# Modulation rows of a two-layer diffusion backbone: up to two per weight granule in four projection blocks, none beside attention

## The chip, the cores and the metric

One core of one Trainium2 chip runs the whole kernel. The metric is the device time of one execution in microseconds (us). TensorE (PE) does the matrix products, VectorE (DVE) and ScalarE (ACT) the elementwise work, GpSimd (POOL) some of it, and SyncE (SP) issues the transfers between HBM and the core's own memory. Each engine works through its own instructions in order, and SP issues its transfers in order.

## The reference

Two layers over 512 latent tokens of width 2048, and 256 context tokens. All data is f32.

```python
m = silu(cond) @ ada_w + ada_b            # adaLN: [2048] x [2048, 3 * 2048]
sh, sc, gt = split(m, 3)
h = rms_norm(x, g) * (1 + sc) + sh
# even layer: one projection h @ w_in into u, v, gates, q, k, v; context gives k and v only
ya = chunk_gmlp(gelu(u), gelu(v)) * silu(ag)         # A: spatial mixing in chunks of 128 tokens
yb = diff_attention(q, [k, kc], [v, vc]) * silu(bg)  # B: 8 heads, two softmaxes each, one subtracted
x = x + gt * (concat(ya, yb) @ w_out)
# odd layer, with its own adaLN: h @ w_in, GLU, depthwise convolution of 31 taps, LayerNorm, gate, w_out
```

The change concerns the adaLN vectors that are not needed at once: the even layer's `gt`, and the odd layer's scale, `sh` and `gt`.

## The kernel before, in words

Every product is taken in three passes, because operands are split into a high half (rounded for TensorE) and a low half (the rest): high by high, high by low, low by high. A **weight granule** is 1 MB of a weight matrix. `load_w` (L98) issues its load on SP into `raw` (three buffers, L94), makes the high half `whi` on ScalarE (L103) and the low half `wlo` on VectorE or GpSimd (L104); each of the two has two buffers, so `whi` of a granule waits until TensorE has left the granule two before it.

The stages, in the names used below:

- **K0**: the first half of K, by 512 columns, while the first adaLN vectors are computed on TensorE and the normalised inputs `hf`, `hcf` are split into `hhi`, `hlo` and `hc`.
- **V0, K1, V1, Q0, Q1**: halves of V, K and Q by `m_block` (L170). Four granules each; K and V have 72 matmuls a granule (latent and context tokens), Q has 48. Each block's results go through `qk_post` (L513: norm and rotation, `ms`, `tn`, `rot`, then a transpose `z` and the split `qkhi`, `qklo`) or `v_post` (L550), and are written to HBM (`k_s`, `v_s`, `q_s`).
- **AV0, AV1**: the gMLP's value half; behind each, `spatial_weights` (L632) transposes four of the eight spatial matrices `wsr` into `z` (L635) and splits them.
- **U**: two groups of `t_group` (L115); behind each, the spatial mixing, whose gated result `mx` (L679) is written to `ug_s` (L680).
- **Attention** (L898 on): 32 turns of scores `S`, maxima, exponentials `e` (L841), transposes `t`, split into `ph` and `pl` (L854, through L111 and L112), and values `oT` (L864). Its order on TensorE is written by hand: 18 granules of the remaining projections (`fill_stream`, L722) are spread between the turns. `load_kq` (L796) loads `kk` and `qq`.
- **Out-projection** and then the odd layer.

**Modulation rows.** The four late vectors are sums over 64 rows of 1 MB (`raw`, 128 x 2048), sixteen for each. `ada_step` (L452) is called by a hook once per granule: it loads a row through `load_raw` and adds it, times a column of `silu_c`, to the sum `acc` on VectorE (L468; the first row of a vector by L466). After the sixteenth, the vector is spread over the partitions (`spread`), turned into columns (`columns`) and, where needed, written out as a row (`row`), one of these at each later call. `hook` takes one row, `hook2` up to two. Before the change the 64 rows lie so: four in each of V0, K1, V1 and Q0, three in Q1, eight in AV, thirteen in U, thirteen beside attention, eleven in the out-projection.

A scheduler puts the instructions of each engine in an order from the program's order and its own estimates; loads and halves of weights get priority (`W_AHEAD`). TensorE's order is written by hand in K0 and attention, SP's in K0.

Of the kernel before, what the change touches and what calls it, by code (L numbers as in the profile page):

```python
# [45 lines left out]
def hybrid_layers_kernel(  # L46
# [43 lines left out]
    y_s = dscr([2, KT, P, T], "y_s")  # L90


    def load_raw(W, r0, nk, c0, ncols):
        raw = wp.tile([P, nk, ncols], F32, tag="raw", bufs=3, name=nm("raw"))  # L94
        SP.dma_start(raw, W[r0 : r0 + nk * P, c0 : c0 + ncols].rearrange("(k p) n -> p k n", p=P))
        return raw

    def load_w(W, r0, nk, c0, ncols, lo_eng=None):  # L98
        with tc.high_priority(offset=W_AHEAD):
            raw = load_raw(W, r0, nk, c0, ncols)  # L100
            hi = wp.tile([P, nk, ncols], F32R, tag="whi", name=nm("whi"))
            lo = wp.tile([P, nk, ncols], F32R, tag="wlo", name=nm("wlo"))
            A.copy(hi, raw)  # L103
            (lo_eng or V).tensor_tensor(lo, raw, hi.bitcast(F32), op=ALU.subtract)  # L104
        return hi, lo
# [256 lines left out]
    def make_hc(kt, Acol, shcol):  # L362
        z = zt(TC)
        for t in range(NTC):
            PE.transpose(z[:, t * P : (t + 1) * P], cch[t][kt // 4][:, (kt % 4) * P : (kt % 4 + 1) * P], ident)
        hcf = tp.tile([P, TC], F32, tag="d", name=nm("hcf"))
        A.activation(hcf, z, AF.Identity, bias=shcol[:, 1:2], scale=Acol[:, 1:2])
        hc = hcp.tile([P, 2, TC], F32R, tag="hc", name=nm("hc"))
        split(hc[:, 0, :], hc[:, 1, :], hcf, V)
        hcm[kt] = (hc[:, 0, :], hc[:, 1, :])  # L370
# [4 lines left out]
    k0ps = [psA.tile([P, 512], F32, tag="m", name=nm("mb")) for _ in range(NT + NTC)]  # L375

    with tc.manual_schedule(engines={mybir.EngineType.PE, mybir.EngineType.SP}):
        wks = {0: load_w(e_w_in, 0, 4, C_K, 512)}
        for q in range(4):
            ada_load(0, q)  # L380
        work = []
# [1 line left out]
        for j in range(NS):  # L383
# [21 lines left out]
            for q in range(4):  # L405
                if j + 1 < NS:
                    ada_load(j + 1, q)
                    if j == 0 and q == 3:
                        load_ctx()
                    if q == 2 and sets[j][-1] % 4 == 3 and sets[j][-1] < KT - 1:  # L410
                        wks[sets[j][-1] // 4 + 1] = load_w(e_w_in, (sets[j][-1] + 1) * P, 4, C_K, 512)
                if q == 3:
                    work += now
                for f in work[: 3 + q % 2]:
                    f()
                del work[: 3 + q % 2]
# [30 lines left out]
    for W, c0, kind in ((e_ada_w, 2 * D, 0), (o_ada_w, D, 1), (o_ada_w, 0, 2), (o_ada_w, 2 * D, 3)):  # L447
        for jt in range(KT):
            ada_jobs.append((W, c0, kind, jt))
    ada_state = {"i": 0, "acc": None}  # L450

    def ada_step(zalloc, n=1):  # L452
        if ada_tail:
            f = ada_tail.pop(0)
            f(zalloc)
            if f.__name__ == "spread":
                return
        for _ in range(n):
            if ada_state["i"] >= len(ada_jobs):
                return  # L460
            W, c0, kind, jt = ada_jobs[ada_state["i"]]
            ada_state["i"] += 1
            raw = load_raw(W, jt * P, 1, c0, D)[:, 0, :]
            if jt == 0:
                ada_state["acc"] = ap_.tile([P, D], F32, tag="acc", name=nm("acc"))
                V.tensor_scalar(ada_state["acc"], raw, sc_[:, 0:1], None, op0=ALU.mult)  # L466
            else:
                V.scalar_tensor_tensor(ada_state["acc"], raw, sc_[:, jt : jt + 1], ada_state["acc"], op0=ALU.mult, op1=ALU.add)  # L468
            if jt == KT - 1:
                ada_tail.extend(ada_finish(kind, ada_state["acc"]))  # L470
                return
# [41 lines left out]
    def qk_post(ps, which, tt, half, tok0, dst, rope):  # L513
# [25 lines left out]
        z = zt()  # L539
        for i in range(4):  # L540
            PE.transpose(z[:, i * P : (i + 1) * P], r[:, i * P : (i + 1) * P], ident)
        hi = tp.tile([P, 4, P], F32R, tag="hi", name=nm("qkhi"))
        lo = tp.tile([P, 4, P], F32R, tag="lo", name=nm("qklo"))
        split(hi, lo, z.rearrange("p (a b) -> p a b", b=P))
        for s, tl in ((0, hi), (1, lo)):
            SP.dma_start(
# [1 line left out]
            )  # L548

    def v_post(ps, half, tok0):  # L550
        hi = tp.tile([P, 4, P], F32R, tag="hi", name=nm("vhi"))
        lo = tp.tile([P, 4, P], F32R, tag="lo", name=nm("vlo"))
        split(hi, lo, ps.rearrange("p (a b) -> p a b", b=P))
        for s, tl in ((0, hi), (1, lo)):
            SP.dma_start(
                v_s[4 * half : 4 * half + 4, s, tok0 : tok0 + P, :].rearrange("h t d -> t h d"), tl.bitcast(F32)
            )
# [9 lines left out]
    def q_done(ps, half):  # L567
        for b in range(NT):
            qk_post(ps[b], 0, b, half, b * P, q_s, True)

    hook, hook2 = (lambda gi, n=n: ada_step(zt, n) for n in (1, 2))
    k_done(k0ps, 0)
    ps = m_block(e_w_in, C_BV, both(), psA, "m", hook)
    v_done(ps, 0)


# [32 lines left out]
        V.tensor_scalar(lam, lam, LAMBDA_INIT, None, op0=ALU.add)  # L609
        V.tensor_scalar(nlam, lam, -1.0, None, op0=ALU.mult)  # L610

    ps = m_block(e_w_in, C_K + 512, both(), psA, "m", hook)
    k_done(ps, 1)
    ps = m_block(e_w_in, C_BV + 512, both(), psA, "m", hook)
    v_done(ps, 1)
    for hb in range(2):
        ps = m_block(e_w_in, C_Q + 512 * hb, lat(), psA, "m", hook)
        q_done(ps, hb)
    p12a.close()

# [21 lines left out]
    for hb in range(2):  # L642
        ps = m_block(e_w_in, C_AV + 512 * hb, lat(), psA, "m", hook)
        for t in range(NT):
            av_ = avt[t][:, 512 * hb : 512 * hb + 512]
            A.activation(av_, ps[t], AF.Gelu)
            junk = bp.tile([P, 512], F32, tag="mx", name=nm("junk"))
            A.activation(junk, av_, AF.Square, accum_out=ssv[:, t, hb : hb + 1])
        spatial_weights(hb)
    vn = []  # L650
    for t in range(NT):
        hi = bp.tile([P, AW], F32R, tag="wv", bufs=9, name=nm("vnh"))
# [5 lines left out]
        V.scalar_tensor_tensor(lo, avt[t], rsv[:, t : t + 1], hi.bitcast(F32), op0=ALU.mult, op1=ALU.subtract)  # L658
        vn.append((hi, lo))

    for ug in range(2):
        ps = t_group(e_w_in, C_U + 512 * ug, hm, psA, "m", hook=hook2)
        for j in range(4):
            g = 4 * ug + j
            gu = bp.tile([P, T], F32, tag="gu", bufs=3, name=nm("gu"))
# [56 lines left out]
    def fill_stream():  # L722
# [10 lines left out]
        for x, (n, gi) in enumerate(grans):  # L733
            kind, i = jobs[n][:2]
            w, nxt = nxt, (load(*grans[x + 1]) if x + 1 < len(grans) else None)
            if gi == 0:
                ps = ps0 if kind == "y" else [None, None]
            if x % 4 != 3:
                ada_step(zt3, 1)
            if (n, gi) == (7, 1):  # L740
                for kt in [0, 1, 2, 3, 4, 5, 8]:
                    y_load(kt)
# [514 lines left out]
```

## Time and profile before

| | us |
|---|---|
| median of three runs | 1892.61 (1892.12 to 1898.86) |
| the profiled execution | 1892.11 |
| its span | 1890.3 |
| TensorE busy | 1819.3 |
| VectorE busy | 1125.1 |
| ScalarE, GpSimd busy | 560.2, 446.7 |
| rows added on VectorE by L468 (60) | 145.2 |

The profile is of one execution; 1.8 us lie around its span. In its rows, a line such as "L468 DVE ... acc<-raw" names the line of the kernel, the engine, the tile written and the tiles read. A bracket at the end of a timeline row tells how long the engine stood idle before the row, and what released it. In the list of waits the numbers are the total in us, the number of waits and the longest. In a row of windows the columns are the window's length, busy us and number of instructions of PE, PE's weight loads, DVE, ACT and POOL, then TensorE's granted clock as a share of full speed, the transfer engines' busy share and GB/s.

### The profile page before, as it was taken

How to read it: one execution, taken by the hardware profiler on the slowest of the kernel's cores; microseconds unless marked ns; L12 is line 12 of the kernel's file. 1: busy time of each engine (PE TensorE's matmuls, PEld its weight loads, DVE VectorE, ACT ScalarE, POOL GpSimd, SP SyncE). 2: the span in 40 equal slices, each digit the busy share in tenths (PEclk: the TensorE clock that was granted, in tenths of full speed). 3: DMA queues.
4: the chain of work that ended last, by engine and by line, in shares of the span. 5: the costliest groups of instructions: out<-in, count | busy, mean ns of one | idle time of the engine just before them, and what ended most of it. 6: DMA issues, size and time to landing. Idle time of an engine off the chain costs nothing.

```text
span 1890.3 us, 21892 instructions
## 1 busy us (share of the span) xinstructions
PE 1819.3 (96%) x8767; PEld 1486.8 (79%) x8767; DVE 1125.1 (60%) x1571; ACT 560.2 (30%) x747; POOL 446.7 (24%) x173
## 2 busy tenths in 40 slices
PE   5999999999999987999999999999999999999998
PEld 2568888888788866877788879888888888888887
DVE  4437436357553645666685555329999999865111
ACT  3332112122331233444343224422222222364110
POOL 0002001011000121323220002135445445444432
PEclk9999999999999998999999999999999999999999
DMA  9996745656763875664676763222332322323441
GB/s 323 339 328 211 220 144 171 197 160 225 249 233 104 319 207 178 186 179 142 203 287 204 252 209 115 89 90 90 99 102 90 106 95 89 101 101 133 141 155 61
DMA packets 208487, 327.34 MB, mean 173 GB/s; under 512 B 10249, under 2 KB 116610, under 8 KB 200194
## 3 DMA queue, kind: packets, MB, share of 16 engines
q1 hardware_dynamic: 208386, 325.94, 53.6%
q8 instruction: 69, 1.13, 0.2%
q14 instruction: 32, 0.26, 0.0%
HBM read 292.33 MB, written 33.58 MB: 172 GB/s over the span
## 4 chain that ended last, share of the span: by engine, by line
PE 75%; DMA 10%; DVE 6%; issue 4%; ACT 2%; POOL 1%; SPq 1%; DVEq 0%; ACTq 0%; POOLq 0%
PE tg L67 28%; PE mb L67 19%; PE m L67 14%; PE fm L67 5%; DMA raw<-in_o_ada_w_dram 4%; DVE acc L468 2%; PE oT L67 2%; DVE wlo L104 2%; PE z L304 2%; PE S L67 2%; ACT whi L103 1%; DMA raw<-in_e_w_in_dram 1%; POOL wlo L104 1%; DMA q_s<-qklo 1%; DMA raw<-in_e_ada_w_dram 1%
## 5 line engine op out<-in xcount | busy, mean ns | idle before, releaser
L104 POOL TENSOR_TENSOR wlo<-raw,whi 128x2048 fp32r<-128x2048 f32 x80 | 369.3, 4616 | 670.2 <-ACT whi L103 662.7
L103 ACT CAST whi<-raw 128x2048 fp32r<-128x2048 f32 x136 | 259.8, 1910 | 720.8 <-PE tg L67 205.4
L1122 DVE SCALAR_TENSOR_TENSOR z<-y,dwc,z 128x512 f32<-128x512 f32 x480 | 319.4, 754 | 0.1
L67 PE MATMUL tg<-h2h,wlo 128*128 128x512 f32 x704 | 274.7, 390 | 0.0
L67 PE MATMUL tg<-h2l,whi 128*128 128x512 f32 x704 | 273.9, 389 | 0.0
L67 PE MATMUL tg<-h2h,whi 128*128 128x512 f32 x704 | 270.8, 389 | 0.0
L468 DVE SCALAR_TENSOR_TENSOR acc<-raw,silu_c,acc 128x2048 f32<-128x2048 f32 x60 | 145.2, 2420 | 132.6 <-DMA raw<-in_o_ada_w_dram 85.0
L104 DVE TENSOR_TENSOR wlo<-raw,whi 128x2048 fp32r<-128x2048 f32 x56 | 128.2, 2290 | 140.5 <-ACT whi L103 140.5
L67 PE MATMUL mb<-whi,hhi 128*128 128x512 f32 x512 | 203.1, 398 | 0.0
L67 PE MATMUL mb<-whi,hlo 128*128 128x512 f32 x512 | 201.6, 394 | 0.0
L67 PE MATMUL mb<-wlo,hhi 128*128 128x512 f32 x512 | 201.5, 394 | 0.0
L67 PEld LDWEIGHTS tg<-h2h,wlo 128*128 128x128 f32 x704 | 132.2, 188 | 27.9 <-issue 0.5
L67 PEld LDWEIGHTS tg<-h2l,whi 128*128 128x128 f32 x704 | 132.2, 188 | 27.9 <-issue 0.5
L67 PEld LDWEIGHTS tg<-h2h,whi 128*128 128x128 f32 x704 | 132.2, 188 | 27.3
L194 POOL TENSOR_TENSOR rs<-ms,mhalf 128x8 f32<-128x8 f32 x20 | 38.2, 1923 | 375.1 <-DVE ms L193 375.1
L67 PEld LDWEIGHTS mb<-whi,hhi 128*128 128x128 f32 x512 | 97.1, 190 | 32.1 <-issue 11.7
L67 PEld LDWEIGHTS mb<-whi,hlo 128*128 128x128 f32 x512 | 97.1, 190 | 20.3
L67 PEld LDWEIGHTS mb<-wlo,hhi 128*128 128x128 f32 x512 | 97.0, 190 | 19.4 <-DVE wlo L104 0.2
L67 PE MATMUL fm<-hhi,whi 128*128 128x512 f32 x256 | 109.3, 427 | 0.0
L67 PE MATMUL fm<-hlo,whi 128*128 128x512 f32 x256 | 102.8, 402 | 0.0
L67 PE MATMUL fm<-hhi,wlo 128*128 128x512 f32 x256 | 102.6, 401 | 0.0
L67 PE MATMUL m<-wlo,y2h 128*128 128x512 f32 x256 | 99.6, 389 | 0.0
(265 smaller groups left out, 3021.6 us busy)
## 6 DMA issues: line engine op xcount, KB each, us to landing
raw<-in_e_w_in_dram SPq DMA_DIRECT2D x56, 1024.0 KB, 5.9
raw<-in_o_ada_w_dram SPq DMA_DIRECT2D x48, 1024.0 KB, 6.2
raw<-in_o_w_in_dram SPq DMA_DIRECT2D x48, 1024.0 KB, 5.1
raw<-in_e_ada_w_dram SPq DMA_DIRECT2D x64, 512.0 KB, 8.0
raw<-in_e_ada_w_dram SPq DMA_DIRECT2D x16, 1024.0 KB, 5.2
raw<-in_e_w_out_dram SPq DMA_DIRECT2D x16, 1024.0 KB, 5.2
raw<-in_o_w_out_dram SPq DMA_DIRECT2D x16, 1024.0 KB, 6.1
qq<-q_s SPq DMA_DIRECT2D x16, 512.0 KB, 7.9
```

Source lines behind the costliest of these rows:

```text
L67: return PE.matmul(o, l, r, start=start, stop=stop)
L103: A.copy(hi, raw)
L104: (lo_eng or V).tensor_tensor(lo, raw, hi.bitcast(F32), op=ALU.subtract)
L194: G.tensor_tensor(dst, tmp, mhalf[:, 0:1].broadcast_to([P, n]), op=ALU.pow)
L304: PE.matmul(ada_ps[j][32 * g : 32 * g + 32, 0 : 2 * nc_], S[:, kt, :], raw[:, i, :], start=(kt < 4), stop=(kt >= KT - 4), skip_group_check ...
L468: V.scalar_tensor_tensor(ada_state["acc"], raw, sc_[:, jt : jt + 1], ada_state["acc"], op0=ALU.mult, op1=ALU.add)
L1122: V.scalar_tensor_tensor(zi if t == TAPS - 1 else z, y2[:, t : t + T], w(t), z, op0=ALU.mult, op1=ALU.add)
```

## The change

`ada_step` is parted into taking a row (`ada_take`, which issues its load) and adding it (`ada_add`). With a pool given, a call first adds the row taken ahead in the call before, then takes and adds its own row, and then takes one more, into a pool `w0` that has a single buffer; that row is added at the next call. `hook0` does so in V0, K1, V1 and Q0; Q1 and AV keep one row a granule, U up to two, and attention has none. V1 has the last sum of the first vector and its steps, so that only two of its granules take two rows. The 64 rows now lie so: eight in V0 and in K1, four in V1, eight in Q0, four in Q1, seven in AV, thirteen in U, none beside attention, twelve in the out-projection.

To find room for `w0`, the high and low halves of `qk_post` and `v_post` share three buffers where they had two each, `rb` is put among them, and `hcf` shares a tag with `hf`. K0's weights load through `w0` as well. `spatial_weights` is called behind the first two granules of the first U group, no longer behind the AV blocks.

```diff
-    def load_raw(W, r0, nk, c0, ncols):
-        raw = wp.tile([P, nk, ncols], F32, tag="raw", bufs=3, name=nm("raw"))
+    def load_raw(W, r0, nk, c0, ncols, pool=None):
+        raw = (pool or wp).tile([P, nk, ncols], F32, tag="raw", bufs=1 if pool else 3, name=nm("raw"))
...
+    w0 = p12a.enter_context(tc.tile_pool(name="w0", bufs=1))
...
-    rb = rp.tile([P, T], F32, name="rb")
+    rb = tp.tile([P, T], F32, tag="hl", bufs=3, name="rb")
...
-        hcf = tp.tile([P, TC], F32, tag="d", name=nm("hcf"))
+        hcf = tp.tile([P, TC], F32, tag="c", name=nm("hcf"))
...
-        wks = {0: load_w(e_w_in, 0, 4, C_K, 512)}
+        wks = {0: load_w(e_w_in, 0, 4, C_K, 512, pool=w0)}
...
+    def ada_take(pool=None):
+        if ada_state["i"] >= len(ada_jobs):
+            return None
+        W, c0, kind, jt = ada_jobs[ada_state["i"]]
+        ada_state["i"] += 1
+        return kind, jt, load_raw(W, jt * P, 1, c0, D, pool)[:, 0, :]
+
+    def ada_add(job):
+        kind, jt, raw = job
+        if ada_state["n"] == 0:
+            ada_state["acc"] = ap_.tile([P, D], F32, tag="acc", name=nm("acc"))
+            V.tensor_scalar(ada_state["acc"], raw, sc_[:, jt : jt + 1], None, op0=ALU.mult)
+        else:
+            V.scalar_tensor_tensor(ada_state["acc"], raw, sc_[:, jt : jt + 1], ada_state["acc"], op0=ALU.mult, op1=ALU.add)
+        ada_state["n"] += 1
+        if ada_state["n"] == KT:
+            ada_state["n"] = 0
+            ada_tail.extend(ada_finish(kind, ada_state["acc"]))
+            return True
+        return False
+
+    def ada_step(zalloc, n=1, pool=None):
         if ada_tail:
             f = ada_tail.pop(0)
             f(zalloc)
             if f.__name__ == "spread":
                 return
+        done = False
+        if ada_state["ahead"]:
+            done = ada_add(ada_state["ahead"])
+            ada_state["ahead"] = None
         for _ in range(n):
-            if ada_state["i"] >= len(ada_jobs):
+            if done or not (job := ada_take()):
                 return
...
+            done = ada_add(job)
+        if pool and not done:
+            ada_state["ahead"] = ada_take(pool)
...
-        hi = tp.tile([P, 4, P], F32R, tag="hi", name=nm("qkhi"))
-        lo = tp.tile([P, 4, P], F32R, tag="lo", name=nm("qklo"))
+        hi = tp.tile([P, 4, P], F32R, tag="hl", bufs=3, name=nm("qkhi"))
+        lo = tp.tile([P, 4, P], F32R, tag="hl", bufs=3, name=nm("qklo"))
...
+    hook0 = lambda gi: ada_step(zt, 1, w0)
...
-    ps = m_block(e_w_in, C_BV, both(), psA, "m", hook)
+    ps = m_block(e_w_in, C_BV, both(), psA, "m", hook0)
...
-    ps = m_block(e_w_in, C_K + 512, both(), psA, "m", hook)
+    ps = m_block(e_w_in, C_K + 512, both(), psA, "m", hook0)
...
-    ps = m_block(e_w_in, C_BV + 512, both(), psA, "m", hook)
+    ps = m_block(e_w_in, C_BV + 512, both(), psA, "m", hook0)
...
-        ps = m_block(e_w_in, C_Q + 512 * hb, lat(), psA, "m", hook)
+        ps = m_block(e_w_in, C_Q + 512 * hb, lat(), psA, "m", hook if hb else hook0)
...
-        spatial_weights(hb)
...
+    def u_hook(gi):
+        if gi < 2:
+            spatial_weights(gi)
+        hook2(gi)
+
     for ug in range(2):
-        ps = t_group(e_w_in, C_U + 512 * ug, hm, psA, "m", hook=hook2)
+        ps = t_group(e_w_in, C_U + 512 * ug, hm, psA, "m", hook=u_hook if ug == 0 else hook2)
...
-            if x % 4 != 3:
-                ada_step(zt3, 1)
```

More of the change, by code (lines that the diff above doesn't have):

```diff
@@ L90, in hybrid_layers_kernel, with load_w @@
     y_s = dscr([2, KT, P, T], "y_s")
-    def load_raw(W, r0, nk, c0, ncols):
-        raw = wp.tile([P, nk, ncols], F32, tag="raw", bufs=3, name=nm("raw"))
+    def load_raw(W, r0, nk, c0, ncols, pool=None):
+        raw = (pool or wp).tile([P, nk, ncols], F32, tag="raw", bufs=1 if pool else 3, name=nm("raw"))
         SP.dma_start(raw, W[r0 : r0 + nk * P, c0 : c0 + ncols].rearrange("(k p) n -> p k n", p=P))
         return raw
-    def load_w(W, r0, nk, c0, ncols, lo_eng=None):
+    def load_w(W, r0, nk, c0, ncols, lo_eng=None, pool=None):
         with tc.high_priority(offset=W_AHEAD):
-            raw = load_raw(W, r0, nk, c0, ncols)
+            raw = load_raw(W, r0, nk, c0, ncols, pool)
             hi = wp.tile([P, nk, ncols], F32R, tag="whi", name=nm("whi"))
@@ L410, in hybrid_layers_kernel @@
                     if q == 2 and sets[j][-1] % 4 == 3 and sets[j][-1] < KT - 1:
-                        wks[sets[j][-1] // 4 + 1] = load_w(e_w_in, (sets[j][-1] + 1) * P, 4, C_K, 512)
+                        wks[sets[j][-1] // 4 + 1] = load_w(e_w_in, (sets[j][-1] + 1) * P, 4, C_K, 512, pool=w0)
                 if q == 3:
@@ L449, in hybrid_layers_kernel @@
             ada_jobs.append((W, c0, kind, jt))
-    ada_state = {"i": 0, "acc": None}
-    def ada_step(zalloc, n=1):
+    ada_state = {"i": 0, "acc": None, "n": 0, "ahead": None}
+    def ada_take(pool=None):
[18 more added lines that the diff above has]
+    def ada_step(zalloc, n=1, pool=None):
         if ada_tail:
@@ L457, in ada_step @@
                 return
+        done = False
+        if ada_state["ahead"]:
+            done = ada_add(ada_state["ahead"])
+            ada_state["ahead"] = None
         for _ in range(n):
-            if ada_state["i"] >= len(ada_jobs):
+            if done or not (job := ada_take()):
                 return
[L461 to L471, printed above, removed]
+            done = ada_add(job)
+        if pool and not done:
+            ada_state["ahead"] = ada_take(pool)
     ada_tail = []
@@ L550, in v_post @@
     def v_post(ps, half, tok0):
-        hi = tp.tile([P, 4, P], F32R, tag="hi", name=nm("vhi"))
-        lo = tp.tile([P, 4, P], F32R, tag="lo", name=nm("vlo"))
+        hi = tp.tile([P, 4, P], F32R, tag="hl", bufs=3, name=nm("vhi"))
+        lo = tp.tile([P, 4, P], F32R, tag="hl", bufs=3, name=nm("vlo"))
         split(hi, lo, ps.rearrange("p (a b) -> p a b", b=P))
```

## The prediction

> **What bounds the kernel now.** I read the page first, then the waits of TensorE, then the groups of VectorE, then the timeline at the waits that cost most, and the windows for the granted clock.
>
> ```profile
> span 1890.3 us, 21892 instructions
> PE 1819.3 (96%) x8767; PEld 1486.8 (79%) x8767; DVE 1125.1 (60%) x1571; ACT 560.2 (30%) x747; POOL 446.7 (24%) x173
> GB/s 323 339 328 211 220 144 171 197 160 225 249 233 104 319 207 178 186 179 142 203 287 204 252 209 115 89 90 90 99 102 90 106 95 89 101 101 133 141 155 61
> ```
>
> PE is busy 1819.3 of 1890.3 us, so at most 71 us of idle time can be won, plus what runs at a lower clock. The change adds no matmul and removes none. So the time can only come from PE's waits and from the clock. These are the waits that the change touches:
>
> ```profile
> PE oT L67 <- DVE pl L112: 17.9, 9, 5.5
> PE S L67 <- issue: 6.0, 1, 6.0
> PE t L879 <- DVE pl L112: 5.2, 3, 3.5
> PE z L635 <- DMA wsr<-in_e_a_ws_dram: 4.0, 1, 4.0
> PE z L67 <- DVE mx L679: 1.4, 1, 1.4
> ```
>
> The first and the third are in attention: PE waits for `pl`, the low half of the transposed probabilities, which VectorE makes. Why `pl` is late, VectorE's timeline shows, with PE's row for the same moment below it:
>
> ```profile
> 717.55 2.35 DVE L468 SCALAR_TENSOR_TENSOR acc<-raw,silu_c,acc 128x2048 f32<-128x2048 f32 x1 [3.41 <-DMA raw<-in_o_ada_w_dram]
> 719.82 0.68 DVE L112 TENSOR_TENSOR pl<-t,ph 128x512 fp32r<-128x512 f32 x1
> ```
> ```profile
> 720.56 0.44 PE L67 MATMUL oT<-pl,vv 128*128 128x256 f32 x1 [4.63 <-DVE pl L112]
> 859.02 1.05 PE L879 MATMUL t<-ones,sq 128*128 128x1 f32 x8 [1.42 <-DVE pl L112]
> ```
>
> VectorE works in order. It sits 3.41 us for a modulation row that has not landed, adds it in 2.35, and only then makes `pl`; PE stands for 4.63. Of the 17.9 + 5.2 = 23.1 us, all but the 1.42 at 859.02 (no row is near it) and some 0.4 of short waits have such an add in front: 21.3 us.
>
> After such waits the clock falls. In the windows the number after the engines is the granted clock:
>
> ```profile
> 500.00:550.00 50.00, 48.05 (x209) 39.74 (x210) 26.15 (x17) 17.80 (x24) 1.06 (x2) 0.97 0.68 235
> 650.00:700.00 50.00, 42.59 (x188) 34.98 (x188) 21.62 (x26) 13.35 (x21) 11.08 (x3) 0.91 0.85 232
> 700.00:750.00 50.00, 39.88 (x203) 34.24 (x202) 29.06 (x43) 17.28 (x31) 10.20 (x3) 0.91 0.64 188
> 800.00:850.00 50.00, 45.76 (x243) 38.74 (x242) 33.04 (x52) 21.14 (x39) 10.20 (x3) 0.97 0.66 186
> 860.00:870.00 10.00, 10.00 (x46) 8.38 (x46) 4.54 (x10) 2.64 (x6) 1.01 (x1) 0.83 0.17 72
> 900.00:950.00 50.00, 48.34 (x245) 40.86 (x245) 35.64 (x57) 19.46 (x36) 11.21 (x4) 0.93 0.72 221
> ```
>
> A window's length times what its clock lacks is time lost: 4.5 us in 700 to 750, 1.5 in 800 to 850 and 3.5 in 900 to 950, together 9.5, all behind waits for rows; 4.5 in 650 to 700 (behind `mx` and behind `S`); 1.5 in 500 to 550 (behind `wsr`). One slow stretch costs about 1.7 us (0.17 of the 10 us at 860), and that one followed a wait of 1.42. The Trainium skill (TensorE: Matmul & The Clock Gate, HAM oscillation) asks only that PE-idle gaps stay under about 3.4 us; the 0.83 behind 1.42 us of idle disagrees with it. I go by the row.
>
> **The change part by part.** *Attention's rows leave.* 13 adds and 13 loads of 1 MB go from 18 granules. `pl` then stands directly behind what PE and ScalarE give it. Gain 21.3 idle + 9.5 clock = 30.8. What is next late there the trace shows only in the one wait that no add caused, 1.42 with 1.7 of clock; I take 4 back for new ones like it. Bounds are 0 and half of the gain, 15. Attention: 27.
>
> *`wsr`'s transposes move* from the AV blocks into the first two U granules. The load stays where it was and has a whole block more to land, so the wait of 4.0 and the clock of 1.5 go: 5.5. Transposes, splits and their number are the same; VectorE has room in U, so I put the move itself at nothing; without that cover the two splits cost PE under 1 each.
>
> *The end of the U groups and the first scores.* SyncE's queue, VectorE and PE there:
>
> ```profile
> 655.01 0.33 SPq L95 DMA_DIRECT2D raw<-in_o_ada_w_dram  x1
> 655.61 0.33 SPq L680 DMA_DIRECT2D ug_s<-mx  x1
> 662.58 1.32 SPq L801 DMA_DIRECT2D kk<-k_s  x2
> ```
> ```profile
> 652.63 2.35 DVE L468 SCALAR_TENSOR_TENSOR acc<-raw,silu_c,acc 128x2048 f32<-128x2048 f32 x1 [1.47 <-DMA raw<-in_o_ada_w_dram]
> 654.90 0.68 DVE L679 TENSOR_TENSOR mx<-z,gu 128x512 f32<-128x512 f32 x1
> ```
> ```profile
> 673.83 1.62 PE L67 MATMUL S<-kk,qq 128*128 128x256 f32 x4 [6.02 <-issue]
> ```
>
> The last `mx` stands behind an add and its 1.47 of waiting, its write behind a row's load; `kk` follows, 7 us after that write. Without the row `mx` comes 1.47 + 2.27 = 3.7 us earlier, and a row of 1 MB (3.1 us at the page's best 339 GB/s) is out of the way of the loads. I take 5 of the 6.02, and the 1.43 of the first `mx`: 6.4, with the 4.5 of clock 10.9. Bounds 4 and 12.
>
> In the program this is, on SyncE before the change, with `mx_4562` the last gate, `raw_4661` and `raw_4766` rows:
>
> ```order
> 233 L95 DMA raw_4655<-in_e_w_in_dram 128x8x256
> 234 L95 DMA raw_4661<-in_o_ada_w_dram 128x2048
> 235 L680 DMA ug_s<-mx_4524 128x512
> 236 L680 DMA ug_s<-mx_4543 128x512
> 237 L95 DMA raw_4760<-in_e_w_in_dram 128x8x256
> 238 L95 DMA raw_4766<-in_o_ada_w_dram 128x2048
> 239 L680 DMA ug_s<-mx_4562 128x512
> 240 L801 DMA kk_4582<-k_s 64x2x768 x2
> ```
>
> After it, with `mx_4615` the last gate:
>
> ```order
> 244 L704 DMA ug_s<-mx_4558 128x512
> 245 L704 DMA ug_s<-mx_4577 128x512
> 246 L95 DMA raw_4807<-in_e_w_in_dram 128x8x256
> 247 L704 DMA ug_s<-mx_4596 128x512
> 248 L704 DMA ug_s<-mx_4615 128x512
> 249 L95 DMA raw_4950<-in_e_w_in_dram 128x8x256
> 250 L823 DMA kk_4635<-k_s 64x2x768 x2
> ```
>
> The rows have left; a weight load now stands ahead of `kk`, and that is why I don't take all 6.02.
>
> *V0 with two rows a granule* is what the change costs. The page gives how long a row takes to land (its last number); below it VectorE's rows show that the start of V0 is full already, and PE's what it waits for there:
>
> ```profile
> raw<-in_o_ada_w_dram SPq DMA_DIRECT2D x48, 1024.0 KB, 6.2
> ```
> ```profile
> 143.94 1.28 DVE L466 TENSOR_SCALAR acc<-raw,silu_c 128x2048 f32<-128x2048 f32 x1
> 147.41 0.69 DVE L112 TENSOR_TENSOR hlo<-hf,hhi 128x512 fp32r<-128x512 f32 x1
> 148.73 2.35 DVE L468 SCALAR_TENSOR_TENSOR acc<-raw,silu_c,acc 128x2048 f32<-128x2048 f32 x1 [0.64 <-DMA raw<-in_e_ada_w_dram]
> 154.11 0.29 DVE L109 CAST hc<-hcf 128x256 fp32r<-128x256 f32 x1
> 156.72 2.34 DVE L468 SCALAR_TENSOR_TENSOR acc<-raw,silu_c,acc 128x2048 f32<-128x2048 f32 x1
> 159.65 0.68 DVE L522 TENSOR_TENSOR tn<-mb,rs 128x512 f32<-128x512 f32 x1
> 160.25 0.67 DVE L518 TENSOR_REDUCE ms<-sq 128x8 f32<-128x512 f32 x1
> 160.85 2.28 DVE L104 TENSOR_TENSOR wlo<-raw,whi 128x2048 fp32r<-128x2048 f32 x1
> ```
> ```profile
> 154.46 0.53 PE L67 MATMUL mb<-whi,hc 128*128 128x512 f32 x1 [0.77 <-DVE hc L109]
> ```
>
> VectorE's order there before the change, from the casts of the last context tile (`hc`) to the low half of V0's second weights (`wlo_1529`):
>
> ```order
> 158 L193 TENSOR_SCALAR ms_1346<-ms_1346 128x8
> 159 L109 CAST hc_1255<-hcf_1253 128x256
> 160 L112 TENSOR_TENSOR hc_1247<-hcf_1245,hc_1247 128x256
> 161 L112 TENSOR_TENSOR hc_1255<-hcf_1253,hc_1255 128x256
> 162 L518 TENSOR_REDUCE ms_1371<-sq_1369 128x8
> 163 L522 TENSOR_TENSOR tn_1301<-mb_330,rs_1297 128x512
> 164 L193 TENSOR_SCALAR ms_1371<-ms_1371 128x8
> 165 L468 SCALAR_TENSOR_TENSOR acc_1524<-raw_1685,silu_c,acc_1524 128x2048
> 166 L530 TENSOR_TENSOR rot_1303<-tn_1301,SG_1291 128x16x16 x2
> 167 L522 TENSOR_TENSOR tn_1326<-mb_331,rs_1322 128x512
> 168 L518 TENSOR_REDUCE ms_1396<-sq_1394 128x8
> 169 L104 TENSOR_TENSOR wlo_1529<-raw_1526,whi_1528 128x2048
> ```
>
> And after it, where `wlo_1534` is that low half:
>
> ```order
> 166 L541 TENSOR_TENSOR tn_1329<-mb_334,rs_1325 128x512
> 167 L549 TENSOR_TENSOR rot_1306<-tn_1304,SG_1294 128x16x16 x2
> 168 L466 SCALAR_TENSOR_TENSOR acc_1527<-raw_1613,silu_c,acc_1527 128x2048
> 169 L549 TENSOR_TENSOR rot_1331<-tn_1329,SG_1294 128x16x16 x2
> 170 L554 TENSOR_TENSOR tn_1304<-tn_1304,CG_1293 128x512
> 171 L466 SCALAR_TENSOR_TENSOR acc_1527<-raw_1694,silu_c,acc_1527 128x2048
> 172 L554 TENSOR_TENSOR tn_1329<-tn_1329,CG_1293 128x512
> 173 L555 TENSOR_TENSOR rot_1306<-rot_1306,tn_1304 128x512
> 174 L537 TENSOR_REDUCE ms_1399<-sq_1397 128x8
> 175 L466 SCALAR_TENSOR_TENSOR acc_1527<-raw_1697,silu_c,acc_1527 128x2048
> 176 L555 TENSOR_TENSOR rot_1331<-rot_1331,tn_1329 128x512
> 177 L104 TENSOR_TENSOR wlo_1534<-raw_1531,whi_1533 128x2048
> ```
>
> Between casts and low half there was one add (row 165); now there are three (168, 171, 175), and a fourth at row 155, four rows ahead of the casts. That fourth waits for a row whose buffer comes free when the low half of V0's first weights is done. The same operations ended with the `hlo` at 148.1 before, with the first add of 1.28 among them; now that add is behind the low half, so it is done at 146.8. With 0.7 for the issue and 6.2 the row lands at 153.7, its add ends at 156.0. From there to `wlo_1534`'s end the new order has eleven operations of some 0.62 (two of them start 0.60 apart at 159.65), 6.8; seven small ones like the casts, 1.5; the low half, 2.3; three adds at 2.27, 6.8; and I allow 0.7 of waiting for a row: 174.1. PE, held by nothing, comes to the first matmul with that low half 40 matmuls and two groups of transposes behind 153.7, by 163.2. So PE idles 10.9 us where it idled 0.77: 10.1 lost, and in pieces of 1.4 to 4, so two to three slow stretches of 1.7: 4. Together 14. Bounds: 5, if rows land early and half of it is hidden; 25, if the four rows land one after the other (four times 6.2, against 10.9 + 3).
>
> *K1, V1 and Q0 with two rows.* Q0's granules are the short ones. ScalarE's casts wait for PE to leave a granule, so they mark its length, and VectorE's rows show how late the low half is:
>
> ```profile
> 344.50 1.91 ACT L103 CAST whi<-raw 128x2048 fp32r<-128x2048 f32 x1 [14.41 <-PE mb L67]
> 371.70 1.91 ACT L103 CAST whi<-raw 128x2048 fp32r<-128x2048 f32 x1 [5.84 <-PE mb L67]
> 382.58 1.91 ACT L103 CAST whi<-raw 128x2048 fp32r<-128x2048 f32 x1 [8.97 <-PE mb L67]
> ```
> ```profile
> 330.13 2.29 DVE L104 TENSOR_TENSOR wlo<-raw,whi 128x2048 fp32r<-128x2048 f32 x1 [1.68 <-ACT whi L103]
> 374.25 2.35 DVE L468 SCALAR_TENSOR_TENSOR acc<-raw,silu_c,acc 128x2048 f32<-128x2048 f32 x1 [4.72 <-DMA raw<-in_e_ada_w_dram]
> 376.52 2.28 DVE L104 TENSOR_TENSOR wlo<-raw,whi 128x2048 fp32r<-128x2048 f32 x1
> ```
>
> A boundary falls at 371.70 and the next at 382.58, so the low half that ends at 376.52 + 2.28 = 378.80 is 3.8 us early; in V1 the one that ends at 332.42 is 12.1 early against 344.50. A second add of 2.35 fits into both. In Q0, a second wait for a row as long as the 4.72 does not: 2.35 + 4.72 - 3.8 = 3.3 us of idle, with a slow stretch 5.0 a granule. The second row stands in SyncE's queue too, and what waits there for its buffer holds the weights' load, V1's writes of `v` and `lv` behind it. Q0 then has to move 4 MB of weights, 8 of rows and V1's 3 of `v` in four granules of 10.9 us: 15 MB in 43.5 us, 345 GB/s, where the page shows 339 at most. Some of it can slip into V1 and Q1. I take 4, near one such granule; bounds 0 and 20 (all four). The Trainium skill (DMA: Bandwidth & Descriptors, Specifications) gives some 358 GB/s of HBM to a core; by it Q0 would fit, and this term would be 0. The trace never reached that rate, so I keep 4.
>
> *Edits with one answer.* K0's weights through their own buffer: that stage moves 323 to 339 GB/s already, so its order changes nothing, 0. The three shared buffers for high and low halves, `hcf` under another tag and `rb` in a shared buffer: their users are the posts of K, V and Q, covered by the 12.1 us of slack; 0, and without that cover a part of V0's term. One row more in the out-projection and the last spread later: 2.35 of VectorE beside matmuls, 0, at worst 2.
>
> Sum: 27 + 5.5 + 10.9 - 14 - 4 = 25.4 us gained. From the profiled execution's 1892.1 that is 1866.7; the median of the runs is 0.5 higher, so 1867.
>
> **The rivals.** *A, the second row stalls the weights.* If the second row's wait stands ahead of the low half in every granule of V0 and Q0, each costs the 5.0 worked out above: 8 x 5.0 = 40 in place of the 4, 1867 + 36 = 1903, slower. It decides from about six granules on, where 43.4 - 14 = 29.4 us of gain are used up. For it speaks the 4.72 with a single row; against it the 12.1 us of slack in V1, which has V0's granule length.
>
> *B, attention finds another wait.* Then half of 30.8 stays, 15.4 in place of 27: 1867 + 12 = 1879. For it speaks the 1.42 without an add; against it, that most turns have no wait at all though VectorE has the same work in them.
>
> *C, Q0 is bound by transfers.* All four granules wait: 20 in place of 4, 1883. For it the 345 against 339 GB/s.
>
> *D, short waits cost no clock.* If the clock falls only behind longer idle times than those that V0 gets, the 4 of clock there are not paid: 1863. The row at 860 speaks against it. This is what the Trainium skill's rule on gaps, named above, would give.
>
> That the rows don't leave attention can't be: in the new order no add stands between its operations.
>
> **How the numbers follow.** Forecast 0.50, A 0.10, B 0.13, C 0.15, D 0.12. A measurement of this kernel can tell about 0.5%, 9.5 us, from no change: faster is below 1883.1, slower above 1902.1. The forecast and D are faster, B by 0.09 of its 0.13, C by 0.08 of 0.15; of A 0.09 is slower. So 0.79 faster, 0.12 same, 0.09 slower. The forecast's own terms (V0 5 to 25, attention 4 less or 11 more lost, Q0) reach from 1850 to 1880; to leave out no more than A, the upper part of C and 0.05 below, the range goes to 1887.
>
> **What would show it.** Right: no add between `pl` and what feeds it, `oT <- pl` and `t <- pl` under 4 us together, no `wsr` wait, `S` waiting for about 1, the windows from 700 to 950 at 0.98 or more; and between 150 and 180 about 11 us of PE idle for `hc`, `z` and `wlo`. Wrong: `mb <- wlo` in Q0 over 10 us (C, and in V0 too, A), or new waits of attention over 10 us (B).

## The result, and the profile after

The changed kernel takes 1863.24 us (median of 4 runs, 1862.00 to 1864.49), against 1892.8 before: a ratio of 0.984 (95% interval 0.982 to 0.986). The forecast was 1867. The profiled execution has a span of 1860.2 us, 30.1 less than before.

```profile
span 1860.2 us, 21958 instructions
PE 1808.0 (97%) x8767; PEld 1478.0 (79%) x8767; DVE 1122.4 (60%) x1571; ACT 560.5 (30%) x747; POOL 451.2 (24%) x173
```

TensorE's waits after the change:

```profile
PE S L67 <- DMA kk<-k_s: 6.3, 1, 6.3
...
PE mb L67 <- DVE hc L109: 3.4, 1, 3.4
PE oT L67 <- DVE pl L112: 2.7, 3, 1.7
...
PE z L560 <- DVE rot L555: 2.3, 1, 2.3
...
PE mb L67 <- DVE wlo L104: 1.5, 1, 1.5
...
PE z L67 <- DVE mx L703: 0.4, 1, 0.4
```

The 23.1 us behind `pl` are 2.7 now, and the wait for `wsr` has left the list. New at V0's start are the waits for `rot` and `wlo`, and the one for `hc` has grown from 0.8 to 3.4; the three are 7.2 us in all. The wait of `S` is as long as it was (6.0); only the releaser has changed its name, from "issue" to the transfer of `kk`. The windows, with the granted clock as the third number from the end:

```profile
500.00:550.00 50.00, 50.00 (x222) 41.30 (x221) 26.46 (x13) 17.13 (x21) 0.00 (x0) 1.00 0.72 257
650.00:700.00 50.00, 43.05 (x209) 36.10 (x207) 15.08 (x23) 15.00 (x18) 18.32 (x4) 0.93 0.88 224
700.00:750.00 50.00, 50.00 (x275) 42.47 (x274) 33.35 (x55) 24.54 (x44) 13.58 (x4) 1.00 0.60 168
...
900.00:950.00 50.00, 48.30 (x274) 41.31 (x274) 32.77 (x53) 23.24 (x41) 11.89 (x4) 1.00 0.69 218
```

From 700 to 950, in attention, the clock is full in every window; before the change it was 0.91 in the first of the two shown and 0.93 in the last. Only 650 to 700 still lacks 0.07 of 50, 3.5 us, behind the wait of `S`. And in VectorE's timeline of an attention turn `pl` now follows the product that stood ahead of the add before:

```profile
718.80 0.68 DVE L731 TENSOR_TENSOR th<-th,ugl 128x512 f32<-128x512 f32 x1
719.50 0.69 DVE L112 TENSOR_TENSOR pl<-t,ph 128x512 fp32r<-128x512 f32 x1
```

### The profile page after: what moved, and what is told of

Read it like the earlier page. It is cut to its first block, busy times and chain, and to the rows that moved or that the text cites. A ratio compares the mean times of both kernels' runs of the same rounds, so it can differ in the third digit from the quotient of the medians.

```text
span 1860.2 us, 21958 instructions
## 1 busy us (share of the span) xinstructions
PE 1808.0 (97%) x8767; PEld 1478.0 (79%) x8767; DVE 1122.4 (60%) x1571; ACT 560.5 (30%) x747; POOL 451.2 (24%) x173
## 4 chain that ended last, share of the span: by engine, by line
PE 81%; DMA 9%; DVE 4%; issue 3%; POOL 1%; ACT 1%; SPq 1%; DVEq 0%; ACTq 0%; POOLq 0%
PE tg L67 30%; PE mb L67 19%; PE m L67 14%; PE fm L67 8%; DMA raw<-in_o_ada_w_dram 2%; PE S L67 2%; PE z L305 2%; DMA raw<-in_e_ada_w_dram 2%; PE oT L67 2%; DVE wlo L104 1%; DVE acc L466 1%; DMA v_s<-vhi 1%; PE t L875 1%; DMA x<-in_x_dram 1%; DMA kk<-k_s 1%
## 5 line engine op out<-in xcount | busy, mean ns | idle before, releaser
L466 DVE SCALAR_TENSOR_TENSOR acc<-raw,silu_c,acc 128x2048 f32<-128x2048 f32 x60 | 141.0, 2350 | 87.6 <-DMA raw<-in_o_ada_w_dram 69.6
L67 PEld LDWEIGHTS tg<-h2h,whi 128*128 128x128 f32 x704 | 132.1, 188 | 27.3
L194 POOL TENSOR_TENSOR rs<-ms,mhalf 128x8 f32<-128x8 f32 x20 | 42.6, 2137 | 378.2 <-DVE ms L193 378.2
```

Source lines behind the costliest of these rows:

```text
L67: return PE.matmul(o, l, r, start=start, stop=stop)
L194: G.tensor_tensor(dst, tmp, mhalf[:, 0:1].broadcast_to([P, n]), op=ALU.pow)
```

## Experiments

The theory was the forecast's: VectorE, in order, stood behind rows that had not landed, and that made `pl` late; the second row in V0 costs some of it back. The rivals: the rows' transfers themselves were the cost; V0's loss comes from the changed buffers; and, for the wait of `S` that did not go, that the loads of `kk` and `qq` take that long whatever stands around them. Medians are of 4 to 10 runs; each ratio is to the kernel before, on the same chip and with its 95% interval. The changed kernel (0.984, 0.982 to 0.986) was timed apart from the experiments, and the kernel before had medians of 1893.1 to 1896.6 us beside them. So some 5 us between an experiment and the changed kernel, and overlapping intervals, are no proof by themselves; there the waits in the traces, of one execution each, carry the argument.

**Attention's rows left out of the kernel before (neither loaded nor added).**

```diff
-    def ada_step(zalloc, n=1):
+    def ada_step(zalloc, n=1, skip=False):
...
-            raw = load_raw(W, jt * P, 1, c0, D)[:, 0, :]
             if jt == 0:
+                ada_state["acc"] = None
+            if skip:
+                pass
+            elif not ada_state["acc"]:
+                raw = load_raw(W, jt * P, 1, c0, D)[:, 0, :]
                 ada_state["acc"] = ap_.tile([P, D], F32, tag="acc", name=nm("acc"))
...
             else:
+                raw = load_raw(W, jt * P, 1, c0, D)[:, 0, :]
...
             if x % 4 != 3:
-                ada_step(zt3, 1)
+                ada_step(zt3, 1, True)
```

> The kernel before, with the thirteen rows beside attention left out: neither loaded nor added (their part of the modulation sums is missing; spreads and columns stay). If the rows beside attention cost what stood behind them (21.3 us of idle TensorE and some 10 of clock, and the late mx at the end of U with its 1.4 and 1.7), the time falls by 31 to 35, to about 1859. If attention finds another wait in their place, by half, to about 1876. The wait of S stays at about 6 in both.

1858.7 us, ratio 0.981 (0.978 to 0.984). TensorE's waits:

```profile
PE t L884 <- DVE pl L112: 4.4, 2, 3.0
...
PE S L67 <- ACT th L779: 1.5, 1, 1.5
PE oT L67 <- DVE pl L112: 1.4, 3, 0.6
```

`oT`'s wait for `pl` is 1.4 for the 17.9 of before: that cost was with the rows. `S`'s wait fell as well, to 1.5, which neither case had said (both had it at about 6), and the time includes that. Two waits stayed, though: 4.4 us at L884 (L879 before, 5.2). One of them is the 3.52 us at 898 before, which the forecast had counted to an add.

**The same rows loaded, but not added.** The edit as above, with the load kept where it was:

```diff
             raw = load_raw(W, jt * P, 1, c0, D)[:, 0, :]
             if jt == 0:
+                ada_state["acc"] = None
+            if skip:
+                pass
+            elif not ada_state["acc"]:
```

> The kernel before, with the thirteen rows beside attention still loaded but not added (their part of the sums is missing). If VectorE's standing in order behind a row that has not landed is the cause, the time is that of the run without loads, within 4 us: about 1861. If the transfers themselves are the cause (13 MB beside the loads of kk, qq and weights), most of the gain is lost: 1875 or more.

1863.6 us, ratio 0.984 (0.981 to 0.986). Its waits of TensorE:

```profile
PE S L67 <- issue: 5.8, 1, 5.8
...
PE t L883 <- DVE pl L112: 4.4, 2, 3.0
```

`oT`'s wait for `pl` has gone with the adds alone (1.2 us are left, further down the list), although the rows still move. So within the turns it is VectorE's order, not the transfers. The 4.9 us between the two medians are close to the 4.3 of `S` (5.8 against 1.5). The intervals overlap, so the times alone don't show it, but the wait does: for `S` the loads do matter.

**The spatial weights' transposes alone.** The kernel before with `spatial_weights` called from the first U group, as in the change.

> The kernel before with one edit alone: the spatial weights' transposes moved to the first two U granules. If the wait for wsr cost 4.0 us and 1.7 of clock, the time falls by 5 to 6, to about 1887. If U has no room for the splits, or the next wait takes over what is won, by 0 to 2.

1889.6 us, ratio 0.997 (0.996 to 0.999), 4.7 less by the medians and 2.8 to 8 by the interval. The wait for `wsr` is gone from its list of waits. The forecast's 5.5 lies inside.

**One row a granule in V0.**

```diff
-    ps = m_block(e_w_in, C_BV, both(), psA, "m", hook0)
+    ps = m_block(e_w_in, C_BV, both(), psA, "m", hook)
...
-        ps = m_block(e_w_in, C_AV + 512 * hb, lat(), psA, "m", hook)
+        ps = m_block(e_w_in, C_AV + 512 * hb, lat(), psA, "m", hook2 if hb else hook)
```

> The changed kernel with one row a granule in V0 again, without a row ahead there; the four rows go to AV1, with up to two a granule. If the second row's adds ahead of the casts and the low half cost V0 its 7.2 us of waits (0.8 before) and 5.1 of clock, the time falls by 8 to 12, to about 1853. If the shared buffers (three for high and low halves, hcf's tag) make those casts late, it stays at 1863 within 2. If AV1 has no room for a second row, it rises.

1855.6 us, ratio 0.979 (0.976 to 0.982), 7.6 less than the changed kernel's 1863.2 by the medians.

```profile
PE mb L67 <- DVE hc L109: 3.4, 1, 3.4
...
PE mb L67 <- DVE wlo L104: 0.9, 1, 0.9
```

The ratios give 8.7; their intervals overlap narrowly. The wait for `rot` is gone, and that for `wlo` in V0 (the 0.9 is in AV1, at 539), but that for `hc` is not, and so the gain is no larger. Nor is all of it V0's: `S` waits 4.5 here, 1.8 less than in the changed kernel. With a single row an add still stands ahead of the casts in VectorE's order: at 153.7, with the casts at 157.3.

**The buffer edits alone, in the kernel before.** `w0` for K0's weights, the shared tags; hooks, rows and `spatial_weights` as before.

> The kernel before with the buffer edits alone: K0's weights through their own buffer, the three shared buffers for high and low halves, hcf's and rb's tags; the rows and the spatial weights where they were. The forecast has this at nothing: 1892 within 3, and the casts of hc waited for by 0.8 us. If these edits, not the second row, make the casts of hc late, the wait for hc is 3.4 and the time 3 to 6 longer.

1893.2 us, ratio 0.998 (0.997 to 1.000), and `hc` waited for by 0.8 as before. The buffers are not V0's cost.

**K0's weights through the shared buffers, in the changed kernel.**

```diff
-        wks = {0: load_w(e_w_in, 0, 4, C_K, 512, pool=w0)}
+        wks = {0: load_w(e_w_in, 0, 4, C_K, 512)}
...
-                        wks[sets[j][-1] // 4 + 1] = load_w(e_w_in, (sets[j][-1] + 1) * P, 4, C_K, 512, pool=w0)
+                        wks[sets[j][-1] // 4 + 1] = load_w(e_w_in, (sets[j][-1] + 1) * P, 4, C_K, 512)
```

> The changed kernel with one edit undone: K0's weights load through the three shared buffers again. If K0's order changes nothing, 1863 within 2, with the wait for hc at 3.4. If the weights' own buffer set the order of VectorE ahead of the casts (the low half of V0's first weights later), the wait for hc goes back to 0.8 and the time falls by 3 to 5.

1864.2 us, ratio 0.984 (0.981 to 0.986), `hc` at 3.4. The time is the same, as forecast, but in this trace as a sum of two changes: V0 has no wait for `rot`, and the clock from 150 to 200 is 0.97, not 0.90; K0 loses about as much, with TensorE busy for 26.3 of the first 50 us (29.3 in the changed kernel) and a clock of 0.91 and 0.95 in the first two windows of 50 us (0.97 and 1.00).

**The adds of V0 behind the last split of `hc`,** with one row a granule and, with `hook0` in place of `hook`, with two (`last_hc` holds VectorE's last split instruction; `issue_after` orders an engine's queue and adds no wait):

```diff
+    def v0_hook(gi):
+        with tc.issue_after(last_hc[0].ins):
+            hook(gi)
+
+    ps = m_block(e_w_in, C_BV, both(), psA, "m", v0_hook)
```

> The run with one row a granule in V0, and there each add queued on VectorE behind the last split of hc. If an add ahead of those casts is what is left of V0's waits (hc 3.4 us and one slow stretch of 1.7), they go and the time is 1850 to 1853, against 1855.6. If the adds only move ahead of rot and the low half, another wait of 1 to 3 us stands there and it stays at 1854 to 1857.

> The changed kernel with two rows a granule in V0 kept, each of its adds queued on VectorE behind the last split of hc. If the place of the adds in VectorE's order, not the number of rows, makes V0's cost, most of its 7.2 us of waits and 5.1 of clock go: 1853 to 1856. If two adds are too much for V0's start wherever they stand, the wait for hc goes and those for rot and the low half grow by as much: 1861 to 1864.

One row: 1859.9 us, ratio 0.983 (0.980 to 0.985); two rows: 1864.2, ratio 0.984 (0.982 to 0.986). With two rows the waits are

```profile
PE mb L67 <- DVE wlo L104: 2.1, 1, 2.1
PE z L561 <- DVE rot L556: 2.0, 1, 2.0
PE mb L67 <- DVE hc L109: 1.3, 1, 1.3
PE mb L67 <- DVE tn L542: 1.1, 1, 1.1
```

`hc` is waited for by 2.1 less, `wlo` by 0.6 more, and 1.1 for `tn`, at 190, is new. The time is that of the second expectation; its waits are so only in part, since `hc` still has 1.3 and `rot` did not grow (2.3 to 2.0). V0's waits fall by 0.7 in all and its clock loses 3.5 us for 5.1, which the times do not show. Moving two adds is no cure, then: most of the cost stays wherever they stand. With one row the wait for `wlo` (2.0) takes what `hc` gave (3.4 to 1.3). The 1859.9 is above both of that run's cases, which no wait in V0 explains; its interval overlaps that of the run with one row and the adds not held back, so no gain is shown.

**`S` eight steps later.**

```diff
-        fill(FP)
+        fill(32)
```

> The changed kernel with the first scores eight steps later in the order of TensorE (32 of the fill steps ahead of them instead of 24, 5.4 us of matmuls more). If the wait of S is the landing of kk and qq, whose time the order doesn't change, it falls from 6.3 to about 1 and its slow stretch goes: 1855 to 1859. If another wait follows it there, or the steps are missed at the end of attention, 1862 or more.

1872.2 us, ratio 0.988 (0.985 to 0.990): 9 slower than the changed kernel by the medians, 8 by the ratios, whose intervals overlap narrowly. That is the second case. `S`'s wait fell to 0.8 as expected, and attention's end pays for it:

```profile
PE oT L67 <- DVE pl L112: 4.8, 4, 2.9
...
PE t L204 <- DVE dg L198: 2.6, 1, 2.6
```

Its window there:

```profile
950.00:1000.00 50.00, 41.58 (x241) 35.80 (x241) 24.31 (x39) 12.74 (x22) 2.77 (x2) 0.83 0.32 111
```

Those steps were the cover of the last head's chain; without them its waits show, and at a clock of 0.83 (1.00 in the changed kernel) the window loses 8.5 us more. A wait can be moved off only if something else covers the place that the cover came from.

**The second head's loads later.** `load_v(0)` and `load_kq(1)` are issued by ScalarE behind the first exponentials:

```diff
-        load_v(0)
         fill(FP)
         scores(*units[0])
         weights(*units[0])
+        with tc.issue_after(last_exp[0].ins):
+            load_v(0, A)
+            load_kq(1, A)
```

> The changed kernel with the second head's kk and qq and the first vv issued by ScalarE behind the first exponentials, no longer by SyncE right behind the first head's kk and qq. If those 2.5 MB crowd the first head's 1.75 MB, S's wait falls from 6.3 to under 2: 1854 to 1860. If the first head's loads take as long by themselves, 1863. If ScalarE's issues hold up the casts of weights, it rises.

1865.4 us, ratio 0.985 (0.981 to 0.989).

```profile
PE S L67 <- DMA qq<-q_s: 5.3, 1, 5.3
```

With 2.5 MB out of the way `S` waits 1 us less, and the time is no lower. The crowd behind the first head's loads is not the cause.

**The weight load ahead of `kk` moved behind it** (`last_q` holds the first head's last load of `qq`).

```diff
+            if x == 3:
+                with tc.issue_after(last_q[0].ins):
+                    w, nxt = nxt, load(*grans[x + 1])
```

> The changed kernel with one weight load moved on SyncE's queue: the one that stands ahead of the first kk now stands behind the first two heads' loads. If that 1 MB is what made the first head's loads land later (16.8 us from the issue of kk to S, 11.2 before the change), S's wait falls from 6.3 to 1 to 3 and the time by 3 to 7, to 1856 to 1860. If the head's own loads take that long, S's wait stays at 5 or more and the time at 1863. If the load comes too late for its granule, a wait for wlo appears between 680 and 720.

1857.65 us, ratio 0.982 (0.979 to 0.985), 5.6 less than the changed kernel by the medians, 3 by the ratios; the intervals overlap, and it is the trace that decides. SyncE's queue in the changed kernel:

```profile
661.31 0.38 SPq L95 DMA_DIRECT2D raw<-in_e_w_in_dram  x1
664.05 1.32 SPq L823 DMA_DIRECT2D kk<-k_s  x2
```
```profile
680.88 2.90 PE L67 MATMUL S<-kk,qq 128*128 128x256 f32 x8 [6.29 <-DMA kk<-k_s]
```

and with the load moved:

```profile
665.43 1.31 SPq L828 DMA_DIRECT2D kk<-k_s  x2
...
675.97 0.54 SPq L95 DMA_DIRECT2D raw<-in_e_w_in_dram  x1
```

```profile
676.41 1.64 PE L67 MATMUL S<-kk,qq 128*128 128x256 f32 x8 [0.63 <-ACT th L801]
```

From `kk`'s issue to `S` it takes 16.8 us in the one and 11.0 in the other, and `S` waits 0.6. The 1 MB that went 2.7 us ahead was the cause, and the slow stretch behind `S` went with it: the clock of this window was 0.66 in the changed kernel.

```profile
680.00:690.00 10.00, 10.00 (x50) 8.37 (x49) 5.64 (x11) 8.18 (x13) 4.39 (x1) 1.00 1.07 268
```

**Both: one row in V0, and that load moved.**

> The run with one row a granule in V0, with the same load moved. If both edits add up, 1849 to 1853; if the load is not the cause, 1855.6 within 2.

1851.1 us, ratio 0.978 (0.976 to 0.981). It lies in the 1849 to 1853 expected if the edits add up, and is the fastest version: 12 us under the changed kernel by the medians, 10 by the ratios, with intervals that do not overlap.

## Why the prediction was right, and where it was not

The total was right within 4 us, the terms less so; errors of both signs cancel, so that it came this near is in part luck. Idle time and clock before and after, from the waits and the windows:

| term | forecast | measured |
|---|---|---|
| attention's rows | +27 | +31.6 |
| `wsr` | +5.5 | +5.5 |
| end of U and `S` | +10.9 | +1.7 |
| V0 | -14 | -11.5 |
| Q0 | -4 | 0 |
| sum | +25.4 | +27.3 |

The measured column is worked out as the forecast was: waits from the list, and what the clock lacks in the windows. For the end of U that is 1.0 of `mx` (1.4 to 0.4), 1.0 of clock (4.5 to 3.5) and 0.3 lost on `S`. The other 2.8 of the span's 30.1 us lie outside the terms: a slow stretch less between 50 and 100 (the clock went from 0.97 to 1.00, 1.5; over the runs it is 0.95 to 1.00), a wait of 1.6 less near 1115, 1.3 more for `dwr`, and 1 that is spread too thin to place. The forecast's reach of "1850 to 1880" adds the good ends of three terms but not their bad ends, which (11 + 11 + 16) would reach 1905; nothing here tests that.

**Attention** was right in its direction: 23.1 us of waits became 2.7, 20.4, and 9.5 + 1.7 of clock came back. The 4 for new waits was not needed; rival B is refuted. For `oT` the mechanism is shown: without adds, its waits go. The changed kernel has one more case of it. "In the new order no add stands between its operations" does not hold in time: rows of the out-projection are added from 938.9 on, before attention's last turns are done, and the longest wait for `pl` that is left stands behind one (`pl` follows it at 941.16).

```profile
938.89 2.35 DVE L466 SCALAR_TENSOR_TENSOR acc<-raw,silu_c,acc 128x2048 f32<-128x2048 f32 x1 [0.48 <-DMA raw<-in_o_ada_w_dram]
```
```profile
941.90 0.39 PE L67 MATMUL oT<-pl,vv 128*128 128x256 f32 x1 [1.70 <-DVE pl L112]
```

For the other two waits, at L879, it is not shown. The forecast put the 3.52 us to an add and kept the 1.42 as one that no row had made; without adds and without rows both are still there, 1.41 and 2.99. So some of the 31.6 is not the adds'. What stands ahead of both waits in the run without rows is a step of the vector that was summed up last, which TensorE takes into the same two buffers `t` (its spread here, its columns at the other):

```profile
822.03 1.07 PE L489 MATMUL t<-acc,ones 128*32 128x512 f32 x8
...
828.83 1.05 PE L884 MATMUL t<-ones,sq 128*128 128x1 f32 x8 [1.41 <-DVE pl L112]
```

With the rows these steps left attention too, for the second U group, and both waits went. That the steps are the cause is not shown; no run moved them alone. At the later wait VectorE's rows show something else as well: a product ahead of `pl` that takes 3.25 us, where the same one takes 0.68 at 855.00 in this run. It began while GpSimd made a low half, and ended 0.56 us after it (863.62 + 4.61 = 868.23):

```profile
863.62 4.61 POOL L104 TENSOR_TENSOR wlo<-raw,whi 128x2048 fp32r<-128x2048 f32 x1 [12.71 <-ACT whi L103]
```
```profile
865.54 3.25 DVE L712 TENSOR_TENSOR th<-th,ugl 128x512 f32<-128x512 f32 x1
```

In the kernel before it is the first row's add that stands there, from 895.01: 4.49 us, where such an add takes 1.28 elsewhere, ending 1.1 after a low half of GpSimd's (893.81 + 4.60). So the 3.52 was not a row that had not landed. But four such products in the changed kernel take 2.7 us too, and TensorE doesn't wait behind them, so this alone doesn't make the wait either.

**The step that failed is "I take 5 of the 6.02"** with its share of 4.5 of clock. The order had shown what would go wrong: "a weight load now stands ahead of `kk`". The issue of `kk` did come earlier against TensorE: 10.5 us ahead of the moment that `S` is wanted (664.05 to 674.59), where it was 5.2 (662.58 to 667.80). But the time from issue to `S` grew from 11.2 to 16.8, because the weight load stood in the way. Before the change the transfer engines had been less than half busy as `kk` was issued, by the last number but one; after it they were full:

```profile
662.50:665.00 2.50, 2.50 (x13) 2.07 (x12) 1.70 (x1) 1.86 (x1) 0.56 (x1) 1.00 0.35 102
```
```profile
660.00:670.00 10.00, 10.00 (x46) 8.29 (x45) 0.00 (x0) 0.77 (x1) 1.28 (x1) 1.00 1.04 289
```

The first window is the kernel before, the second the changed one. The gain of being 5.3 earlier was lost as 5.6 of later landing, and with the load moved the wait is gone.

**V0** was right in its place and in the order of VectorE, and partly lucky in its times. VectorE's rows in the changed kernel, with the adds between the casts of `hc` and the low half:

```profile
151.30 1.36 DVE L537 TENSOR_REDUCE ms<-sq 128x8 f32<-128x512 f32 x2 [0.52 <-ACT sq L534]
...
152.65 2.35 DVE L466 SCALAR_TENSOR_TENSOR acc<-raw,silu_c,acc 128x2048 f32<-128x2048 f32 x1
156.19 0.48 DVE L109 CAST hc<-hcf 128x256 fp32r<-128x256 f32 x2
...
159.47 2.34 DVE L466 SCALAR_TENSOR_TENSOR acc<-raw,silu_c,acc 128x2048 f32<-128x2048 f32 x1
...
163.01 2.34 DVE L466 SCALAR_TENSOR_TENSOR acc<-raw,silu_c,acc 128x2048 f32<-128x2048 f32 x1
...
167.08 2.33 DVE L466 SCALAR_TENSOR_TENSOR acc<-raw,silu_c,acc 128x2048 f32<-128x2048 f32 x1
...
169.94 2.28 DVE L104 TENSOR_TENSOR wlo<-raw,whi 128x2048 fp32r<-128x2048 f32 x1
```

The add ahead of the casts began at 152.65 (forecast 153.7), and the low half ended at 172.2 (174.1), behind three more adds as the order had them. But the forecast had that first add wait for its row, and its row shows no wait: what VectorE waited for was `sq`, ahead of `ms`, and the add followed. The low half was 1.9 earlier than forecast, and TensorE came 1.9 later to it (165.1 without its idle time, for 163.2), after a first slow stretch that cost 1.8; so 10.9 of idle became 7.2. The forecast counted idle time and clock side by side, while the one hides some of the other. 7.2 us of idle less 0.8 is 6.4, and 5.1 of clock makes 11.5 for the forecast's 14. The clock, in the windows of V0's start:

```profile
150.00:160.00 10.00, 6.47 (x25) 4.75 (x24) 9.37 (x21) 3.30 (x6) 7.18 (x4) 0.88 0.91 342
160.00:170.00 10.00, 7.89 (x35) 6.25 (x33) 10.00 (x11) 3.60 (x4) 3.31 (x1) 0.94 0.67 221
170.00:180.00 10.00, 8.36 (x26) 6.54 (x27) 7.89 (x15) 0.58 (x1) 3.27 (x2) 0.66 0.97 308
```

How far is the second row the cause? `wlo`'s wait of 1.5 to 2.1 is in every run with two rows in V0, and with one row it is gone unless the add is held back behind `hc`. `rot`'s wait goes with one row, but it is also absent with two rows when K0's weights load through the shared buffers, so the order matters there too. For `hc` it is not shown: with one row, too, an add stands ahead of its casts, where the run with the buffer edits alone has it at 149.8, long done. Both have one row in V0, and the scheduler has ordered them differently; why was not tried.

**Q0** cost nothing: from 360 to 404 TensorE was busy throughout.

```profile
360.00:404.00 44.00, 44.00 (x196) 36.32 (x195) 32.76 (x21) 9.27 (x10) 0.00 (x0) 1.00 1.01 362
```

The forecast took 339 GB/s for the most, from slices of 47 us; a 44 us stage moved 362. Its 345 GB/s was also a slip of units: its 15 MB are 15 times 1024 KB, so 15.7 million bytes, and 362 GB/s in 43.5 us. The Trainium skill (DMA: Bandwidth & Descriptors, Specifications) gives about 358 GB/s of HBM to a core. The trace's 362 agrees with it to 1%. By an estimate from the Trainium skill's figure, the 15.7 million bytes take 43.9 us, 0.4 more than the 43.5, so with the sum put right the term by it would have been near 0. Rival C falls with this row, and so does A's part in Q0; in V0 the only wait for the low half is the 1.5, not A's 5.0 in each of four granules.

**Rival D**, short waits cost no clock, is refuted in V0: behind the waits of 2.3 and 1.5 the clock of the window from 170 is 0.66, 3.4 us lost. But no length decides alone. Behind the 1.70 at 941.9 in the changed kernel it stays at 1.00 (900 to 950 above), and of two waits of 1.41 at the same place, in the runs without rows and without adds, one has a slow stretch behind it and the other none:

```profile
830.00:840.00 10.00, 10.00 (x47) 8.32 (x47) 4.60 (x11) 2.64 (x6) 1.01 (x1) 0.84 0.18 63
```
```profile
830.00:840.00 10.00, 8.59 (x46) 6.96 (x45) 5.50 (x11) 2.42 (x6) 4.12 (x2) 1.00 0.38 124
840.00:850.00 10.00, 10.00 (x57) 8.39 (x56) 5.16 (x10) 4.74 (x8) 0.00 (x0) 1.00 0.39 138
```

The first fence is the run without rows (the wait ends at 828.8), the second the run without adds (it ends at 834.6). The Trainium skill's limit of about 3.4 us for gaps (TensorE: Matmul & The Clock Gate, HAM oscillation) is no safe bound here; no run shows what else decides.

## What to carry to other kernels

An in-order engine that waits for a transfer holds back everything behind it, so work that nobody waits for belongs where the engine has slack and its data has landed; where the engine is full, at the start of V0, the same work costs what it saved elsewhere. When a change empties one queue, look at what moves up in it: here a weight load of 1 MB moved ahead of the loads that the next stage waits for, and took back all that their earlier issue had won. Two edits can also cancel in the time and show only in the trace, as K0 and V0 did in one run here. A sum of terms can be right for wrong reasons, so check each term in the profile after, not only the total.

## What was not expected of the hardware

The same 1.4 us of idle TensorE was followed by a slow stretch in one run and not in another.

Some of VectorE's instructions do not get done while GpSimd makes a low half: the products of `th` and `ugl`, and the adds of rows. In the kernels before and after and in the runs without rows and without adds, each of the 15 products of `th` and `ugl` that began during a low half ended 0.54 to 0.56 us after it, whatever its length (1.67 to 3.25 us, where it takes 0.68 otherwise); two adds did so 2.14 to 2.15 us after it. Others go on: `th` times `fm` took its 0.68 at 864.82, within such a low half. That the two engines share something is inferred from these rows; no run took GpSimd's low halves away.

A stage with weights, rows and writes together moved 362 GB/s over 44 us, while the loads of `kk` and `qq`, into 64 partitions each, fill the transfer engines at some 215 GB/s. The row is of the run with the second head's loads later, where neither these nor `vv` are under way: a share of 1.07 at 219 GB/s.

```profile
672.00:676.00 4.00, 4.00 (x20) 3.29 (x18) 0.00 (x0) 0.93 (x1) 2.99 (x1) 1.00 1.07 219
```
